# Convolution taps over five 64-token segments in two sums, sigmoids by tanh, and weight splits queued later at the second norm

## The chip, the core and the metric

The kernel runs on one core of a Trainium2 chip. The metric is the device time of one execution in microseconds (us). A core has a matrix engine (TensorE, PE in the profile, with its weight loads as PEld), VectorE (DVE), ScalarE (ACT), GpSimd (POOL) and a queue that starts transfers (SyncE, SP). Each engine runs its own instructions strictly in the order in which they were queued, and waits on semaphores for the others.

## The reference

One layer of a streaming encoder, for a prompt of 256 tokens and a running stream of 64 tokens that share the weights:

```python
h = rmsnorm(x, g_pre_mix);  p = h @ w_in
# head group A, 1024 channels: Conformer convolution
u = h_val * sigmoid(h_gate)
u = causal depthwise conv over positions, width 31 (w_dw, b_dw)   # prompt after zeros, stream after its state
u = silu(LayerNorm per token over each group of 128 channels)
# head group B, 8 heads of 128: gated DeltaNet (short conv of width 4, l2norm, beta = sigmoid(b_raw), delta rule in chunks of 64)
x = x + rmsnorm(concat(A, B) @ w_out)
h = rmsnorm(x);  gu = causal depthwise conv (width 3) of h @ w_up
x = x + rmsnorm((silu(gate) * up) @ w_down)
```

It also returns the convolution states (the last 30 rows of `u` among them) and the delta-rule states.

## The kernel before

Activations lie with channels on the 128 partitions and the 320 tokens (256 + 64) on the free axis. Every matrix product is done in three passes of 128x128 weights on 320 tokens: high part of the weight by high part of the activation (L212), high by low (L213), low by high (L216). The parts come from `split_w` (L192): a DMA lands 128x1024 weights in a buffer `w`, ACT copies it to `whi` (L196) and DVE subtracts to `wlo` (L197). There are three buffers each of `w`, `whi` and `wlo`.

The program is traced as one stream of dense matrix blocks. Small work is spread between them: `tick` counts dense matmuls, and every 20 (`GAP`) it resumes generators ("jobs": convolution tails, head tails, `pair` with `levels` and `post`) and takes up to `pace` convolution steps from the list `taps`. A list scheduler then orders each engine's queue by priorities, data and the `issue_after` edges; so an edit in one place also moves neighbours.

What the change touches:

- `gates` (L398): `beta` is a Sigmoid on ACT (L414).
- `conv_block` (L503), run eight times (c0 to c7): the gate block's `sg` is scaled on DVE (L508), goes through Sigmoid on ACT (L509) and is multiplied by `rb` on POOL (L510). The values go to `ub`, one row of 380 columns: 30 border columns, 256 tokens, 30 state columns (L515), 64 tokens. The 31 taps run over 350 of these columns. Tap 0 is on ACT (L525); taps 1 to 30 are one DVE instruction each that reads `cvt` and writes it again (L526), so each needs the result of the one before.
- `conv_tail` (L532): PE transposes `cvt` (`pt_c`, L541), DVE takes statistics (L543, L544), POOL the power (L547), DVE `gnm` (L549), ACT normalises into `un` (L552).
- `levels` (L731): PE forms `pz` (L741), DVE masks it into `zs` (L743), PE goes on with `px` from `zs` (L747). PE's queue holds L747 at a fixed place among the dense matmuls, so PE stands still if `zs` is late.
- the second norm (L1020 to L1042): after the last block of `w_out`, PE sums squares (L235), DVE and POOL make the root (`rr`, L240, L241), PE spreads it (L248) into `psb`, and fills the time with matmuls of zeros (`keep_warm`, L256). Then for each of 16 feature blocks k DVE does `m[k] * rb1` (L1036) and adds it to `x1` (L1037), ACT makes `hi2[k]` (L1041) and DVE `lo2[k]` (L1042); PE starts the first up-projection group (`up_group`, L1051) with block 0. The weights of that group are split by `up_weights` (L987), eight tiles of two blocks each, in between. In L1028 the third of these splits is tied behind `held`, an ACT instruction, only.

Of the kernel before, what the change touches and what calls it, by code (L numbers as in the profile page):

```python
# [12 lines left out]
ALU = mybir.AluOpType  # L13
# [88 lines left out]
def trunk_kernel(ctx, tc, ins, outs):  # L102
# [295 lines left out]
    def gates():  # L398
# [12 lines left out]
        S.copy(ba, ps3[:, :, 0:16])  # L411
        V.tensor_tensor(ba, ba, ps3[:, :, 16:32], ALU.add)
        beta = const.tile([P, 3, NH], F32, tag="beta", name="beta")
        S.activation(beta, ba[:, :, 0:8], AF.Sigmoid)  # L414
        gt = const.tile([P, 3, NH], F32, tag="gt", name="gt")
        dtb = gpar[:, 8:16].unsqueeze(1).to_broadcast((P, 3, NH))
        ax = small.tile([P, 3, NH], F32, tag="ax", bufs=1, name="ax")
# [74 lines left out]
    ubufs = [cb.tile([P, 380], F32, tag=f"ub{i}", bufs=1, name=f"ub{i}") for i in range(3)]
    for u in ubufs:
        G.memset(u[:, 0:30], 0.0)
# [8 lines left out]
    def conv_block(b):  # L503
        psg_ = in_block(8 + b, "psgate")
        ub = ubufs[b % 3]
        with tc.high_priority(offset=PRI_E):
            sg = cb.tile([P, T], F32, tag="sg", name="sg")
            V.tensor_tensor(sg, psg_[:, 0:T], rb, ALU.mult)  # L508
            S.activation(sg, sg, AF.Sigmoid)  # L509
            G.tensor_tensor(sg, sg, rb, ALU.mult)  # L510
        psv = in_block(b, "psv")
        if b > 2:
            finish_conv(b - 3)
        with tc.high_priority(offset=PRI_E):
            G.tensor_copy(ub[:, 286:316], pv("s_conv", b * 30, (b + 1) * 30))  # L515
            V.tensor_tensor(ub[:, 30:286], psv[:, 0:TP], sg[:, 0:TP], ALU.mult)
            V.tensor_tensor(ub[:, 316:380], psv[:, TP:T], sg[:, TP:T], ALU.mult)
        nc.sync.dma_start(outs["conv"][:, b, 0, :], ub[:, 256:286])
        nc.sync.dma_start(outs["conv"][:, b, 1, :], ub[:, 350:380])
        cvt = cb.tile([P, 350], F32, tag="cvt", bufs=3, name="cvt")  # L520
        left = [31]

        def tap(t):
            if t == 0:
                return lambda: S.activation(cvt, ub[:, 0:350], AF.Identity, scale=pv("w_dw", b * 31), bias=pv("b_dw", b))  # L525
            return lambda: V.scalar_tensor_tensor(cvt, ub[:, t:t + 350], pv("w_dw", b * 31 + t), cvt, ALU.mult, ALU.add)  # L526

        lefts[b] = left
        taps.extend((left, tap(t)) for t in range(31))
        return cvt, left  # L530

    def conv_tail(b, cvt, left):  # L532
        while left[0]:
            yield GAP, 0, 0
        yield LAG_CONV, 0, 1
        pt = ps_t.tile([P, 512], F32, tag="t", name="pt_c")
        st = cb.tile([P, 3, 6], F32, tag="bst", name="bst")
        gv = cb.tile([P, 3, 2], F32, tag="gvar", name="gvar")

        for c, o in enumerate((0, 128, 222)):  # L540
            PE.transpose(pt[:, c * P:(c + 1) * P], cvt[:, o:o + P], cv("ident"))  # L541
        for c in range(3):
            V.bn_stats(st[:, c, :], pt[:, c * P:(c + 1) * P])  # L543
            V.bn_aggr(gv[:, c, :], st[:, c, :])  # L544
        rs = cb.tile([P, 3], F32, tag="grs", name="grs")
        G.tensor_scalar(rs, gv[:, :, 1], EPS, None, ALU.add)
        G.tensor_tensor(rs, rs, nhalf[:, 0:3], ALU.pow)  # L547
        nm = cb.tile([P, 3], F32, tag="gnm", name="gnm")
        V.scalar_tensor_tensor(nm, gv[:, :, 0], -1.0, rs, ALU.mult, ALU.mult)  # L549
        un = cb.tile([P, 3, P], F32, tag="un", bufs=1, name="un")  # L550
# [471 lines left out]
    with tc.high_priority(offset=PRI_E):  # L1022
# [2 lines left out]
        keep_warm(psw, 5, mm)  # L1025
        rb1, mm = rstd_rows(rr)
        keep_warm(psw, 10, mm)
        with tc.issue_after(held):  # L1028
            upw.append(up_weights(2))
        for k in range(KB):  # L1030
            if k % 2 == 1 and 3 <= k < 13:
                upw.append(up_weights(len(upw)))
            with ExitStack() as e:
                if 0 < k < 4:
                    e.enter_context(tc.issue_after(added))
                V.tensor_tensor(m[k], m[k], rb1, ALU.mult)  # L1036
# [230 lines left out]
```

## Time and profile before

| | us |
|---|---|
| median of 3 runs | 1509.7 (1509.48 to 2070.93) |
| the profiled execution, its own time | 1506.6 |
| span of its trace | 1504.8 |
| PE busy in the span | 1490.6 |
| DVE busy | 1009.6 |
| ACT busy | 734.9 |
| POOL busy | 275.9 |

Busy time of PE is modelled and its matmuls overlap, so its share alone doesn't say how much is lost; the places where it stood idle, and the clock it was granted, do. Stage by stage: input projections with convolution and delta rule up to about 442 us, output projection to 552, second norm and first up-projection group to about 588, feed-forward to 1490, and a tail.

### The profile page before, as it was taken

The page shows a single profiled execution, that of the slowest core. Times are in us where ns is not written, and L with a number is a line of the kernel's source. Part 1 is how long each engine was busy: PE and PEld are TensorE (multiplying, and loading weights), DVE is VectorE, ACT ScalarE, POOL GpSimd, SP SyncE. Part 2 cuts the span into 40 slices and gives each one's busy share as a digit, 9 for nine tenths or more (in the row PEclk, how much of TensorE's full clock was granted, in tenths as well). Part 3 has the DMA queues.
Part 4 walks back from the last instruction along what each step waited for, and adds up shares of the span by engine and source line. Part 5 has one row for each costly group of instructions (what it writes and reads, how often), then busy time and mean ns, then how long its engine had stood idle before and what let it go on. Part 6 is the DMA issues. An engine that isn't in the chain of part 4 may idle for free.

```text
span 1504.8 us, 26707 instructions
## 1 busy us (share of the span) xinstructions
PE 1490.6 (99%) x10330; PEld 1469.6 (98%) x10330; DVE 1009.6 (67%) x1852; ACT 734.9 (49%) x1223; POOL 275.9 (18%) x459
## 2 busy tenths in 40 slices
PE   9999999999999999999999999999999999999998
PEld 9999999989999989999999999999999999999997
DVE  6798898879987578865435666545665545666554
ACT  7663656554555565544344444334444333444453
POOL 0322122330110000322002322001322101322101
PEclk9999999999999999999999999999999999999999
DMA  8435453445334653444555444455444455444453
GB/s 294 150 114 153 140 158 102 125 154 147 118 105 144 201 187 127 141 154 133 144 159 166 144 152 142 135 153 172 142 154 151 126 153 173 144 152 154 128 152 117
DMA packets 98279, 224.25 MB, mean 149 GB/s; under 512 B 18792, under 2 KB 39528, under 8 KB 98152
## 3 DMA queue, kind: packets, MB, share of 16 engines
q1 hardware_dynamic: 98008, 222.51, 47.5%
q8 instruction: 81, 1.33, 0.4%
q14 instruction: 46, 0.38, 0.1%
q10 hardware_dynamic: 144, 0.03, 0.0%
HBM read 215.39 MB, written 7.12 MB: 148 GB/s over the span
## 4 chain that ended last, share of the span: by engine, by line
PE 88%; DVE 6%; DMA 2%; ACT 2%; POOL 1%; issue 1%; ACTq 0%; DVEq 0%; SPq 0%; POOLq 0%
PE psu L212 13%; PE psu L213 13%; PE psu L216 13%; PE psdn L212 6%; PE psdn L213 6%; PE psdn L216 6%; PE psq L212 2%; PE psq L216 2%; PE psq L213 2%; DVE wlo L197 2%; DVE cvt L526 2%; PE psu L1060 2%; PE ps_first L374 1%; PE psgate L216 1%; PE psv L212 1%
## 5 line engine op out<-in xcount | busy, mean ns | idle before, releaser
L196 ACT CAST whi<-w 128x1024 fp32r<-128x1024 f32 (+2 forms) x440 | 412.2, 940 | 502.1 <-PE psu L213 170.1
L197 DVE TENSOR_TENSOR wlo<-w,whi 128x1024 fp32r<-128x1024 f32 (+2 forms) x440 | 477.3, 1085 | 187.1 <-ACT whi L196 114.1
L212 PE MATMUL psu<-hi,whi 128*128 128x320 f32 x1344 | 397.0, 309 | 0.0
L213 PE MATMUL psu<-lo,whi 128*128 128x320 f32 x1344 | 396.9, 309 | 0.0
L212 PEld LDWEIGHTS psu<-hi,whi 128*128 128x128 f32 x1344 | 252.3, 188 | 0.0
L213 PEld LDWEIGHTS psu<-lo,whi 128*128 128x128 f32 x1344 | 252.3, 188 | 0.0
L216 PE MATMUL psu<-hi,wlo 128*128 128x320 f32 x1344 | 224.4, 309 | 0.0
L1093 POOL COPY nffn<-fbuf 128x2 f32<-128x2 f32 x88 | 99.4, 1129 | 587.5 <-DVE fbuf L1091 583.0
L216 PEld LDWEIGHTS psu<-hi,wlo 128*128 128x128 f32 x1344 | 204.1, 188 | 0.0
L213 PE MATMUL psdn<-gl,whi 128*128 128x320 f32 x660 | 195.9, 310 | 0.0
L1091 DVE TENSOR_TENSOR fbuf<-psu,rb 128x256 f32<-128x256 f32 x88 | 37.4, 424 | 169.1 <-PE psu L216 169.0
L212 PE MATMUL psdn<-gh,whi 128*128 128x320 f32 x480 | 142.8, 309 | 0.0
L526 DVE SCALAR_TENSOR_TENSOR cvt<-ub,par,cvt 128x350 f32<-128x350 f32 x240 | 136.7, 587 | 2.9 <-ACT cvt L525 0.3
L213 PEld LDWEIGHTS psdn<-gl,whi 128*128 128x128 f32 x660 | 123.9, 188 | 0.3
L212 PE MATMUL psq<-hh,whi 128*128 128x320 f32 x352 | 106.1, 315 | 0.0
L213 PE MATMUL psq<-hl,whi 128*128 128x320 f32 x352 | 104.1, 309 | 0.0
L212 PEld LDWEIGHTS psdn<-gh,whi 128*128 128x128 f32 x480 | 90.1, 188 | 0.0
L216 PE MATMUL psdn<-gh,wlo 128*128 128x320 f32 x480 | 89.8, 309 | 0.0
L216 PEld LDWEIGHTS psdn<-gh,wlo 128*128 128x128 f32 x480 | 75.4, 188 | 0.0
L212 PEld LDWEIGHTS psq<-hh,whi 128*128 128x128 f32 x352 | 66.1, 188 | 0.3
L213 PEld LDWEIGHTS psq<-hl,whi 128*128 128x128 f32 x352 | 66.1, 188 | 0.2
L1136 DVE TENSOR_TENSOR y<-y,psdn 128x320 f32<-128x320 f32 x45 | 22.0, 489 | 58.4 <-PE psdn L216 58.4
(356 smaller groups left out, 2503.0 us busy)
## 6 DMA issues: line engine op xcount, KB each, us to landing
w<-in_w_up SPq DMA_DIRECT2D x176, 512.0 KB, 3.8
w<-in_w_in SPq DMA_DIRECT2D x88, 512.0 KB, 3.7
w<-in_w_down SPq DMA_DIRECT2D x64, 384.0 KB, 3.1
w<-in_w_down SPq DMA_DIRECT2D x64, 320.0 KB, 2.9
w<-in_w_out SPq DMA_DIRECT2D x32, 320.0 KB, 3.2
w<-in_w_out SPq DMA_DIRECT2D x16, 384.0 KB
w<-in_w_first SPq DMA_DIRECT2D x6, 512.0 KB, 5.8
wtp<-wsp SPq DMA_DIRECT2D x4, 640.0 KB
```

What stands on the lines that cost most here:

```text
L196: S.copy(hi[:, 0:width], w[:, 0:width])
L197: V.tensor_tensor(lo[:, 0:width], w[:, 0:width], hi[:, 0:width].bitcast(F32), ALU.subtract)
L212: tick(PE.matmul(ps, wh, xh, start=(first and k0 + j == 0), stop=False))
L213: tick(PE.matmul(ps, wh, xl, start=False, stop=False))
L216: tick(PE.matmul(ps, lo[:, j * P:(j + 1) * P], xh, start=False, stop=(final and k0 + j == nk - 1)))
L374: tick(PE.matmul(ps, w, xh, start=(k == 0 and wt is hi), stop=(k == KB - 1 and wt is lo)))
L526: return lambda: V.scalar_tensor_tensor(cvt, ub[:, t:t + 350], pv("w_dw", b * 31 + t), cvt, ALU.mult, ALU.add)
L1060: PE.matmul(pss[i][:, 0:T], wt[:, o:o + P], x, start=(k == 0 and n == 0), stop=(k == KB - 1 and n == 2))
L1091: V.tensor_tensor(buf[:, 2:258], psu[:, 0:TP], rb2[:, 0:TP], ALU.mult)
L1093: G.tensor_copy(nffn[:, b, 0, :], buf[:, 256:258])
L1136: V.tensor_tensor(y[:, n, :], y[:, n, :], psd[:, 0:T], ALU.add)
```

## The change

**Taps.** `ub` becomes five segments of 94 columns, 30 of border and 64 of tokens. One DVE instruction writes all five token parts, and a new POOL copy writes the borders of segments 1 to 3 from the ends of segments 0 to 2. Each tap covers 5x64 = 320 columns. Even taps add into `cvt`, odd taps into a new tile `odd` (one buffer); tap 1 is a plain multiply, and a 32nd step adds the two.

**Sigmoids.** `sigmoid(x)` becomes `0.5 * tanh(x / 2) + 0.5`: ACT computes Tanh, and a new POOL instruction scales and shifts, for `beta` and for each `sg` (now with one buffer).

**Second norm.** The splits of up-projection tiles 2, 3 and 4 are queued behind `lo2` of blocks 0, 2 and 4; those of tiles 5 to 7 stand at blocks 7, 9 and 11.

```diff
-        S.activation(beta, ba[:, :, 0:8], AF.Sigmoid)
+        S.activation(beta, ba[:, :, 0:8], AF.Tanh, scale=0.5)
+        G.tensor_scalar(beta, beta, 0.5, 0.5, ALU.mult, ALU.add)
...
-    ubufs = [cb.tile([P, 380], F32, tag=f"ub{i}", bufs=1, name=f"ub{i}") for i in range(3)]
+    ubufs = [cb.tile([P, 5, 94], F32, tag=f"ub{i}", bufs=1, name=f"ub{i}") for i in range(3)]
...
-            S.activation(sg, sg, AF.Sigmoid)
+            S.activation(sg, sg, AF.Tanh, scale=0.5)
+            G.tensor_scalar(sg, sg, 0.5, 0.5, ALU.mult, ALU.add)
             G.tensor_tensor(sg, sg, rb, ALU.mult)
...
-            G.tensor_copy(ub[:, 286:316], pv("s_conv", b * 30, (b + 1) * 30))
-            V.tensor_tensor(ub[:, 30:286], psv[:, 0:TP], sg[:, 0:TP], ALU.mult)
-            V.tensor_tensor(ub[:, 316:380], psv[:, TP:T], sg[:, TP:T], ALU.mult)
+            G.tensor_copy(ub[:, 4, 0:30], pv("s_conv", b * 30, (b + 1) * 30))
+            V.tensor_tensor(ub[:, :, 30:94], psv[:, 0:T].rearrange("p (s i) -> p s i", s=5),
+                            sg.rearrange("p (s i) -> p s i", s=5), ALU.mult)
+            G.tensor_copy(ub[:, 1:4, 0:30], ub[:, 0:3, 64:94])
...
-        left = [31]
+        cvt = cb.tile([P, 5, 64], F32, tag="cvt", bufs=3, name="cvt")
+        odd = cb.tile([P, 5, 64], F32, tag="odd", bufs=1, name="odd")
+        left = [32]
 
         def tap(t):
+            if t == 31:
+                return lambda: V.tensor_tensor(cvt, cvt, odd, ALU.add)
+            x, acc, w = ub[:, :, t:t + 64], (cvt, odd)[t % 2], pv("w_dw", b * 31 + t)
             if t == 0:
-                return lambda: S.activation(cvt, ub[:, 0:350], AF.Identity, scale=pv("w_dw", b * 31), bias=pv("b_dw", b))
-            return lambda: V.scalar_tensor_tensor(cvt, ub[:, t:t + 350], pv("w_dw", b * 31 + t), cvt, ALU.mult, ALU.add)
+                return lambda: S.activation(acc, x, AF.Identity, scale=w, bias=pv("b_dw", b))
+            if t == 1:
+                return lambda: V.tensor_scalar(acc, x, w, None, ALU.mult)
+            return lambda: V.scalar_tensor_tensor(acc, x, w, acc, ALU.mult, ALU.add)
...
-        with tc.issue_after(held):
-            upw.append(up_weights(2))
+        split = None
         for k in range(KB):
-            if k % 2 == 1 and 3 <= k < 13:
-                upw.append(up_weights(len(upw)))
+            if k % 2 == 1 and k < 13:
+                with ExitStack() as e:
+                    if k < 7:
+                        e.enter_context(tc.issue_after(split))
+                        e.enter_context(tc.issue_after(held))
+                    upw.append(up_weights(len(upw)))
...
-            V.scalar_tensor_tensor(lo2[k], x1[:, k, :], g, hi2[k].bitcast(F32), ALU.mult, ALU.subtract)
+            split = V.scalar_tensor_tensor(lo2[k], x1[:, k, :], g, hi2[k].bitcast(F32), ALU.mult, ALU.subtract).ins
```

In ACT's queue 18 of 27 loads of a function table go. PE keeps the same instructions in other places; DVE gets eight `tensor_scalar` and eight adds for eight taps and eight multiplies less; POOL gets 17 instructions more.

How the queues move, at three places. First DVE ahead of the mask of the third pair's `levels`, before (`qb` is a head's short convolution with its taps in `cq`, `psq` its matrix block):

```order
L526 SCALAR_TENSOR_TENSOR cvt<-ub_584,par,cvt 128x350 x4
L587 TENSOR_TENSOR qb_591<-psq,rb 128x256
L588 TENSOR_TENSOR qb_591<-psq,rb 128x64
L543 BN_STATS bst<-pt_c 128x6 x2
L544 BN_AGGR gvar<-bst 128x2
L543 BN_STATS bst<-pt_c 128x6
L594 SCALAR_TENSOR_TENSOR cq<-qb_591,par,cq 128x323
L544 BN_AGGR gvar<-bst 128x2 x2
L594 SCALAR_TENSOR_TENSOR cq<-qb_591,par,cq 128x323
L549 SCALAR_TENSOR_TENSOR gnm<-gvar,grs 128x3
L197 TENSOR_TENSOR wlo<-w,whi 128x1024
L594 SCALAR_TENSOR_TENSOR cq<-qb_591,par,cq 128x323
L743 TENSOR_TENSOR zs<-pz,cst 128x20x16
```

and after, in the same queue (L537 is the tap, L754 the mask; the line numbers of the changed file are higher by 11 here):

```order
L537 SCALAR_TENSOR_TENSOR cvt<-ub_584,par,cvt 128x320
L598 TENSOR_TENSOR qb_591<-psq,rb 128x256
L599 TENSOR_TENSOR qb_591<-psq,rb 128x64
L197 TENSOR_TENSOR wlo<-w,whi 128x1024
L605 SCALAR_TENSOR_TENSOR cq<-qb_591,par,cq 128x323
L537 SCALAR_TENSOR_TENSOR odd<-ub_584,par,odd 128x320
L605 SCALAR_TENSOR_TENSOR cq<-qb_591,par,cq 128x323
L537 SCALAR_TENSOR_TENSOR cvt<-ub_584,par,cvt 128x320
L605 SCALAR_TENSOR_TENSOR cq<-qb_591,par,cq 128x323
L754 TENSOR_TENSOR zs<-pz,cst 128x20x16
```

Five taps, `cvt` and `odd` in turn, stand ahead of the `qb` rows instead of four; behind them the statistics and `gnm` of a convolution tail have moved behind the mask, and two taps have come in. On PE the three transposes `pt_c` of that tail, ahead of `pz` before, now stand among the `px` of L747.

Second, ACT in the output projection, before (`whi` copies, `un` of a convolution tail, `m` the copies out of finished blocks):

```order
L955 COPY m6_5655<-psm_5591 128x320
L196 CAST whi_5761<-w_5759 128x640
L552 ACTIVATE un_5694<-pt_c_5677,gnm_5692,grs_5689 128x128 x3
L955 COPY m7_5732<-psm_5657 128x320
L196 CAST whi_5789<-w_5787 128x768
```

and after:

```order
L966 COPY m6_5673<-psm_5609 128x320
L196 CAST whi_5779<-w_5777 128x640
L196 CAST whi_5807<-w_5805 128x768
L966 COPY m7_5750<-psm_5675 128x320
L196 CAST whi_5835<-w_5833 128x640
L563 ACTIVATE un_5742<-pt_c_5725,gnm_5740,grs_5737 128x128 x3
```

The three `un` have moved behind two `whi` copies and `m7`.

Third, DVE at the second norm, before:

```order
L240 TENSOR_SCALAR rr_6650<-pst_6643 128x3
L197 TENSOR_TENSOR wlo_6675<-w_6672,whi_6674 128x1024
L1036 TENSOR_TENSOR m0_5254<-m0_5254,psb_6658 128x320
L197 TENSOR_TENSOR wlo_6699<-w_6696,whi_6698 128x1024
L1037 TENSOR_TENSOR x1_6131<-x1_6131,m0_5254 128x320
L1036 TENSOR_TENSOR m1_5333<-m1_5333,psb_6658 128x320
L197 TENSOR_TENSOR wlo_6717<-w_6714,whi_6716 128x1024
L1042 SCALAR_TENSOR_TENSOR lo2_0_6681<-x1_6131,par_81,hi2_0_6680 128x320
```

and after:

```order
L240 TENSOR_SCALAR rr_6675<-pst_6668 128x3
L1050 TENSOR_TENSOR m0_5272<-m0_5272,psb_6683 128x320
L1051 TENSOR_TENSOR x1_6156<-x1_6156,m0_5272 128x320
L1050 TENSOR_TENSOR m1_5351<-m1_5351,psb_6683 128x320
L1051 TENSOR_TENSOR x1_6156<-x1_6156,m1_5351 128x320
L1050 TENSOR_TENSOR m2_5403<-m2_5403,psb_6683 128x320
L1056 SCALAR_TENSOR_TENSOR lo2_0_6700<-x1_6156,par_81,hi2_0_6699 128x320
L197 TENSOR_TENSOR wlo_6706<-w_6703,whi_6705 128x1024
L1056 SCALAR_TENSOR_TENSOR lo2_1_6712<-x1_6156,par_81,hi2_1_6711 128x320
```

The three `wlo` that stood ahead of `lo2` of block 0 now come one behind each of `lo2` 0, 2 and 4; from there on every pair of blocks has one `wlo` in it until the eighth tile, where before the pairs between blocks 1 and 9 had none. ACT's three `whi` copies of these tiles stay ahead of `hi2` of block 0.

## Rows read from the trace of the kernel before

**Rows 1.** The page: busy us, share of the span and instructions of each engine.

```profile
PE 1490.6 (99%) x10330; PEld 1469.6 (98%) x10330; DVE 1009.6 (67%) x1852; ACT 734.9 (49%) x1223; POOL 275.9 (18%) x459
```

**Rows 2.** Waits of PE: us in total, times, longest.

```profile
PE px L747 <- DVE zs L743: 3.3, 2, 2.8
PE psm L212 <- ACT whi L196: 1.3, 1, 1.3
PE pks L670 <- ACT vh L662: 1.0, 1, 1.0
PE psm L1009 <- DVE wlo L197: 0.8, 1, 0.8
PE psu L1060 <- ACT hi L1041: 0.6, 1, 0.6
```

**Rows 3.** Windows: length, busy us (count) of PE, PEld, DVE, ACT, POOL, granted clock, DMA.

```profile
322.90:325.50 2.60, 2.60 (x20) 2.60 (x21) 2.53 (x4) 2.58 (x4) 0.00 (x0) 0.82 0.80 239
325.50:328.00 2.50, 2.50 (x11) 2.50 (x11) 2.02 (x5) 0.06 (x1) 0.00 (x0) 0.50 0.48 170
...
442.00:500.00 58.00, 56.74 (x392) 56.44 (x391) 40.25 (x80) 28.67 (x55) 5.76 (x13) 1.00 0.49 145
```

**Rows 4.** Timeline of DVE ahead of that wait: start, length, instruction, idle before.

```profile
302.17 0.59 DVE L526 SCALAR_TENSOR_TENSOR cvt<-ub,par,cvt 128x350 f32<-128x350 f32 x1
302.67 0.56 DVE L594 SCALAR_TENSOR_TENSOR cq<-qb,par,cq 128x323 f32<-128x323 f32 x1
...
307.87 1.82 DVE L526 SCALAR_TENSOR_TENSOR cvt<-ub,par,cvt 128x350 f32<-128x350 f32 x3
...
314.77 2.43 DVE L526 SCALAR_TENSOR_TENSOR cvt<-ub,par,cvt 128x350 f32<-128x350 f32 x4
317.12 0.42 DVE L587 TENSOR_TENSOR qb<-psq,rb 128x256 f32<-128x256 f32 x1
317.46 0.21 DVE L588 TENSOR_TENSOR qb<-psq,rb 128x64 f32<-128x64 f32 x1
317.59 0.48 DVE L543 BATCH_NORM_STATS2 bst<-pt_c 128x6 f32<-128x128 f32 x2
...
322.29 0.48 DVE L743 TENSOR_TENSOR zs<-pz,cst 128x320 f32<-128x320 f32 x1
```

**Rows 5.** Line L510 on POOL and the table load of L509: min/median/max ns.

```profile
L510 POOL TENSOR_TENSOR sg<-sg,rb x8: 862/1036/3268, 81.2 to 420.9; 128x320 f32<-128x320 f32 x8
L509 ACT ACT_TABLE_LOAD   x8: 1283/1283/1283, 79.4 to 419.1; - x8
```

**Rows 6.** Timeline around the wait of the output projection, 466 to 481 us.

```profile
469.36 0.49 PE L541 MATMUL pt_c<-cst,cvt 128*128 128x128 f32 x3
...
476.62 1.16 ACT L552 ACTIVATE un<-pt_c,gnm,grs 128x128 f32<-128x128 f32 x3 [5.27 <-DVE gnm L549]
...
477.97 2.22 ACT L196 CAST whi<-w 128x768 fp32r<-128x768 f32 x3
```

**Rows 7.** Timeline of the second norm, 545 to 566 us.

```profile
554.46 2.32 PE L256 MATMUL psw<-wz 128*128 128x512 bf16 x10
554.66 0.49 DVE L1036 TENSOR_TENSOR m<-m,psb 128x320 f32<-128x320 f32 x1
555.06 1.22 DVE L197 TENSOR_TENSOR wlo<-w,whi 128x1024 fp32r<-128x1024 f32 x1
556.20 0.48 DVE L1037 TENSOR_TENSOR x<-x,m 128x320 f32<-128x320 f32 x1
...
556.72 0.56 ACT L1041 ACTIVATE hi<-x,par 128x320 fp32r<-128x320 f32 x1 [1.46 <-DVE x L1037]
...
558.13 0.55 DVE L1042 SCALAR_TENSOR_TENSOR lo<-x,par,hi 128x320 fp32r<-128x320 f32 x1
558.60 0.48 DVE L1037 TENSOR_TENSOR x<-x,m 128x320 f32<-128x320 f32 x1
```

**Rows 8.** The chain in order of time: the rest of the first up-projection group.

```profile
559.73 26.68 PE psu L1060 x180
```

More of the change, by code (lines that the diff above doesn't have):

```diff
@@ L489, in trunk_kernel @@
     nqkv = const.tile([P, 24, 2, 3], F32, tag="nqkv", name="nqkv")
[L492 removed]
+    ubufs = [cb.tile([P, 5, 94], F32, tag=f"ub{i}", bufs=1, name=f"ub{i}") for i in range(3)]
     for u in ubufs:
[L494 removed]
+        G.memset(u[:, 0, 0:30], 0.0)
     def finish_conv(b):
@@ L514, in conv_block @@
         with tc.high_priority(offset=PRI_E):
-            G.tensor_copy(ub[:, 286:316], pv("s_conv", b * 30, (b + 1) * 30))
-            V.tensor_tensor(ub[:, 30:286], psv[:, 0:TP], sg[:, 0:TP], ALU.mult)
-            V.tensor_tensor(ub[:, 316:380], psv[:, TP:T], sg[:, TP:T], ALU.mult)
-        nc.sync.dma_start(outs["conv"][:, b, 0, :], ub[:, 256:286])
-        nc.sync.dma_start(outs["conv"][:, b, 1, :], ub[:, 350:380])
-        cvt = cb.tile([P, 350], F32, tag="cvt", bufs=3, name="cvt")
-        left = [31]
+            G.tensor_copy(ub[:, 4, 0:30], pv("s_conv", b * 30, (b + 1) * 30))
+            V.tensor_tensor(ub[:, :, 30:94], psv[:, 0:T].rearrange("p (s i) -> p s i", s=5),
+                            sg.rearrange("p (s i) -> p s i", s=5), ALU.mult)
+            G.tensor_copy(ub[:, 1:4, 0:30], ub[:, 0:3, 64:94])
+        for i in range(2):
+            nc.sync.dma_start(outs["conv"][:, b, i, :], ub[:, 3 + i, 64:94])
+        cvt = cb.tile([P, 5, 64], F32, tag="cvt", bufs=3, name="cvt")
+        odd = cb.tile([P, 5, 64], F32, tag="odd", bufs=1, name="odd")
+        left = [32]
         def tap(t):
+            if t == 31:
+                return lambda: V.tensor_tensor(cvt, cvt, odd, ALU.add)
+            x, acc, w = ub[:, :, t:t + 64], (cvt, odd)[t % 2], pv("w_dw", b * 31 + t)
             if t == 0:
-                return lambda: S.activation(cvt, ub[:, 0:350], AF.Identity, scale=pv("w_dw", b * 31), bias=pv("b_dw", b))
-            return lambda: V.scalar_tensor_tensor(cvt, ub[:, t:t + 350], pv("w_dw", b * 31 + t), cvt, ALU.mult, ALU.add)
+                return lambda: S.activation(acc, x, AF.Identity, scale=w, bias=pv("b_dw", b))
+            if t == 1:
+                return lambda: V.tensor_scalar(acc, x, w, None, ALU.mult)
+            return lambda: V.scalar_tensor_tensor(acc, x, w, acc, ALU.mult, ALU.add)
         lefts[b] = left
-        taps.extend((left, tap(t)) for t in range(31))
-        return cvt, left
+        taps.extend((left, tap(t)) for t in range(32))
+        return cvt.rearrange("p s i -> p (s i)"), left
     def conv_tail(b, cvt, left):
@@ L538, in conv_tail @@
         gv = cb.tile([P, 3, 2], F32, tag="gvar", name="gvar")
-        for c, o in enumerate((0, 128, 222)):
+        for c, o in enumerate((0, 128, 192)):
             PE.transpose(pt[:, c * P:(c + 1) * P], cvt[:, o:o + P], cv("ident"))
```

2 lines of the change are left out of this document (1 added, 1 removed).

## The prediction

> **What bounds the kernel now.** The first view is the page's busy time: PE is busy for 1490.6 of 1504.8 us [rows 1], and the change takes no instruction off it. A dense matmul costs 26.68 / 180 = 0.148 us from start to start [rows 8], so time can come or go only where PE stands still or runs at a lower clock. The second view, the waits of PE, names those places; with the first up-projection group they come to some 7 us [rows 2]: 3.3 us for the masks `zs` of `levels` (one wait of 2.8), 1.3 and 0.8 us in the output projection, 1.0 us in a head's tail, 0.6 us at the second norm. The third view, windows, adds the clock. [...] That makes 0.36 x 2.6 = 0.94 us and 2.5 us at half clock, and half of it is lost: **1.7 us**. So everything that can be won is about 9 us, 0.6% of the time. About 2% is what a measurement of this kernel can tell from no change, so whichever way the details go, the result should count as no change; the rest is about its size.
>
> **The taps.** DVE, not PE, is what the 2.8 us wait hangs on, so I follow its queue there [rows 4]. Three taps in a row take 1.82 us and four take 2.43: 0.61 us for each further one. A tap followed by an instruction that doesn't read its result costs only 302.67 - 302.17 = 0.50 us. The difference of 0.11 us is what waiting for the own result costs. The nearest row to a tap of 320 columns is `lo` at the second norm, also two tensors and a per-channel number: 558.60 - 558.13 = 0.47 us to an independent successor [rows 7]. With two sums a tap always follows one of the other sum, so I take 0.47; if two sums didn't help it would be about 0.61 - 0.03 = 0.58. That the 320 columns now lie in five pieces I cost at nothing: the mask `zs`, in pieces of 16 columns, takes 0.48 us for 320 columns [rows 4], no more than plain ones (0.48, rows 7).
>
> Now the queue to `zs`. The three taps ahead of 314.77 save 2 x 0.14 + 0.03 = 0.31 us. The four taps, 317.12 - 314.77 = 2.35 us, become five: 5 x 0.47 = 2.35, no difference. So the first `qb` row moves from 317.12 to 316.81. After it stand two `qb` rows (0.34 and 0.13), one `wlo` (556.20 - 555.06 = 1.14, rows 7), and then three `cq` and two taps, in turn, at 0.47 each: 0.34 + 0.13 + 1.14 + 2.35 = 3.96, so `zs` starts at 320.77 instead of 322.29, 1.5 us sooner. The statistics and the `gnm` of the convolution tail, which stood in between, now come later. So do three transposes on PE (0.49 for three, rows 6, about 0.4 from start to start), which came before the wait and now come behind it: the net gain is **1.1 us**, and the wait left is 2.8 - 1.5 + 0.4 = 1.7 us. Whether the clock still falls decides 1.7 us more. The wait of 2.8 was followed by the fall; the window of 442 to 500, which holds the wait of 1.3, shows 1.00 [rows 3]. 1.7 is nearer to 1.3 than to 2.8, so I take the clock to stay up: **1.7 us**, with none as the other end.
>
> The wait of 1.0 in a head's tail goes through `tq`, POOL and ACT, with three taps ahead of it on DVE: **0.3 us**. For the other 0.5 us of `zs` (3.3 - 2.8) I take nothing: four taps there become five, and a product for a head's output, which reads PE's result, has moved ahead of the mask; 0.5 either way.
>
> In the output projection ACT has waited 5.27 us for `gnm` when it starts three `un` at 476.62, and the `whi` that PE needs comes only at 477.97 [rows 6]: that is PE's 1.3 [rows 2]. In the changed queue that `whi` and one more stand ahead of the `un`, and nothing they need comes from DVE. **1.2 us**, between 0 (if the next `whi` behind `un` is late instead) and 1.3. The 0.8 us of L1009 hangs on a weight transfer; its place in SP's queue shifts by a position or so, which I cost at 0, with 0.8 either way.
>
> **The sigmoids.** A table load is 1.28 us [rows 5]; 18 of them are 23 us of ACT, which is busy half the time, and PE's waits on ACT are the two above. The new POOL instruction reads one tensor of 320 columns; L510, which reads two, takes 0.86 to 3.27 us [rows 5], the nearest row, and I take its median of 1.04. So `sg` is ready between 1.28 - 0.86 = 0.4 us sooner and 2.0 later. What hides it is the value block of 48 matmuls between `sg` and its use, 7.1 us; without that cover eight blocks would cost up to 16 us. On the path: **0**. The border copy on POOL is a new wait for tap 0 on ACT and tap 1 on DVE. Behind tap 0 stand `whi` copies, behind tap 1 the `wlo` and the work of the heads, which PE takes some microseconds later; if POOL is free it is short, and I take 0. It is the dearest risk (rival 2).
>
> L510's 3.27 us against a median of 1.04 [rows 5] shows that POOL can be held up; which instruction held it the row doesn't say. [...]
>
> **The second norm.** Before, DVE puts a `wlo` between `m[0]` and its addition: they start at 554.66 and 556.20, and `hi` starts at 556.72 and takes 0.56 [rows 7]. Without the `wlo` the addition starts 0.40 us behind `m[0]`, at 555.06, and `hi` at 555.06 + 0.52 = 555.58, done by 556.14. But PE's ten zero matmuls run from 554.46 to 556.78 [rows 7], so block 0 starts at about 556.6 instead of 557.3: 0.7 us. Then a pair of blocks costs PE 24 x 0.148 = 3.55 us, and DVE four steps at 0.40, two `lo` at 0.47 and one `wlo` at 1.14, 3.68 us: six pairs in a row lose 6 x 0.13 = 0.8 us, of which some 0.3 is covered by DVE's lead at the start. Net **0.2 us**, between 0.7 won and 0.6 lost (ACT's `whi` copies, 1.03 us each, now stand between the `hi` as well, and wait for a buffer that PE frees). SP's loads of the tiles behind it start later, when the splits free their buffers, but each tile is needed 3.55 us after the one before.
>
> **Sum.** 1.1 + 1.7 + 0.3 + 1.2 + 0.2 = 4.5 us. The profiled execution would take 1506.6 - 4.5 = 1502.1 us. The median lies 3.1 us above it; I put the change on the median: 1509.7 - 4.5 = **1505.2 us**.
>
> **Rivals.** 1. Two sums don't help: a tap costs 0.58, `zs` starts at 314.46 + 5 x 0.58 + 0.47 + 1.14 + 5 x 0.5 = 321.5, 0.8 us sooner; the net gain is 0.4, the wait left 2.4, and the clock falls as before. The sum is 0.4 + 1.2 + 0.2 = 1.8, and the time 1507.9. For it: nothing but this difference of 0.11 us in a few rows. [...]
>
> 2. Slower: the border copy. POOL serves in order, and where the copy stands behind a head's powers or the two `sg` steps, tap 0 waits for it on ACT with a `whi` behind it. At L510's longest, 3.27 us, less the lead of a `whi` (one tile, 24 x 0.148 = 3.55 us, of which casting and subtracting take 2.2), PE stands 1.9 us per block. It decides from a copy that is more than 1.4 us late; in five of eight blocks it costs 9.5 us, and 1509.7 - 4.5 + 9.5 = 1514.7. Against it: POOL is busy 275.9 of 1504.8 us [rows 1].
>
> 3. The other waits fall too: 0.5 of `zs`, 0.8 of L1009, all of the 1.0, and the 1.7 left: 4 us more, 1501.
>
> 4. The change doesn't do what it says at the second norm: DVE falls further behind and PE waits for `hi` from block 6 on, 1 us lost instead of 0.2 won: 1506.4. It lies within the forecast's own range.
>
> **Chances.** Forecast with rival 4, 1503 to 1507: 0.5. Rival 1, 1507 to 1510: 0.22. Rival 3, below 1503: 0.13. Rival 2, above 1510: 0.15. Leaving out the lower part of rival 3 and the upper part of rival 2, the range is **1500.5 to 1512.5**. None of the cases comes near 30 us: faster by over 2% 0.01, within 2% 0.97, slower by over 2% 0.02.
>
> **What would show it.** Taps on DVE 0.47 us apart; the wait of L747's successor near 320 us down to about 1.7, with a granted clock of 1.00 behind it; no wait of PE for `whi` at 477; the first block of the up-projection 0.7 us sooner behind the zero matmuls, and short waits for `hi` from block 6 on. The forecast is wrong if the clock still falls, if taps stay near 0.6 us apart, or if PE shows waits for `whi` or `wlo` behind the first taps of a block.

## The result and the profile after

| | before | after |
|---|---|---|
| median of the runs taken together (us) | 1510.53 (10 runs) | 1515.03 (10 runs) |
| the profiled execution, its own time | 1506.6 | 1512.55 |
| span of its trace | 1504.8 | 1510.8 |
| mean granted clock of the runs | 0.9975 (35 other runs) | 0.9952 |

The ratio is 1.0029, with an interval of 1.0020 to 1.0037: the changed kernel is 0.3% slower. One of the ten runs before took 2070.9 us and is left out of the ratio. The forecast was 0.3% faster, and its range ended at 1512.5. That 2% is what can be told from no change, as the prediction had it, is too coarse: the interval tells 0.3%. A mean clock lower by 0.0023 over 1512 us is 3.5 us lost, so by this estimate most of the 4.5 us is time at half clock.

The page's busy time, as in [rows 1]:

```profile
PE 1494.7 (99%) x10329; PEld 1472.2 (97%) x10330; DVE 1000.3 (66%) x1852; ACT 712.9 (47%) x1205; POOL 306.3 (20%) x476
```

DVE and ACT have 9 and 22 us less to do than before, POOL 30 more, and yet PE waits longer. The waits of PE (us in total, times, longest), to be held against [rows 2]:

```profile
PE px L758 <- DVE zs L754: 5.6, 2, 3.3
PE pks L681 <- ACT vh L673: 1.6, 1, 1.6
PE psw L256 <- POOL wz L226: 1.3, 1, 1.3
PE psm L212 <- ACT bh L220: 0.8, 1, 0.8
```

The wait for the mask `zs` was 3.3 us in all and is 5.6: the third `levels` waits 3.3 where 1.7 was forecast, and the fourth, which was put at no change, waits 2.3. The windows behind these two waits (columns as in [rows 3]):

```profile
324.00:326.30 2.30, 1.90 (x18) 1.90 (x19) 2.30 (x4) 1.48 (x3) 0.30 (x1) 1.00 0.48 185
326.30:329.70 3.40, 3.40 (x16) 3.40 (x16) 2.41 (x11) 0.00 (x0) 1.29 (x3) 0.50 0.51 154
397.50:404.90 7.40, 7.40 (x34) 7.40 (x35) 6.68 (x11) 1.82 (x4) 2.63 (x2) 0.54 0.20 71
404.90:430.00 25.10, 25.10 (x225) 23.99 (x225) 23.20 (x49) 10.93 (x21) 3.34 (x5) 1.00 0.33 101
```

The granted clock is 0.50 behind the first wait, for 3.4 us, and 0.54 in the mean behind the second, for 7.4 us. At the lower clock dense matmuls start 0.27 us apart (403.62, 403.89, 404.15, 404.42), at 1.00 behind it 0.15 (404.90, 405.05, 405.19). By the mean clock the first time costs 1.7 us, as before (0.50 from 324.6 to 328.0 there); the second is new and costs 7.4 x 0.46 = 3.4 us. Comparing the start of the same dense matmul in both traces, the changed kernel is behind by 0.4 us at 115 us, 1.1 at 318, 1.8 at 330, 1.9 at 390, 5.5 at 410, 7.4 at 436, 7.1 at 470, 5.9 at 500, 5.1 at 545, 4.1 at 560 and 5.9 from 620 to the end (times of the kernel before). So 3.6 us arise at the fourth `levels`, 1.9 between 410 and 436 (1.6 of it where PE waits for `bh` and `bl`), and 3.0 are given back between 470 and 560.

Why is the mask of the fourth `levels` late? DVE ahead of it, in the timeline:

```profile
382.69 1.23 DVE L197 TENSOR_TENSOR wlo<-w,whi 128x1024 fp32r<-128x1024 f32 x1 [2.27 <-ACT whi L196]
383.83 0.15 DVE L560 SCALAR_TENSOR_TENSOR gnm<-gvar,grs 128x3 f32<-128x3 f32 x1
383.90 0.54 DVE L536 TENSOR_SCALAR odd<-ub,par 128x320 f32<-128x320 f32 x1
384.35 0.54 DVE L537 SCALAR_TENSOR_TENSOR cvt<-ub,par,cvt 128x320 f32<-128x320 f32 x1
...
395.56 0.55 DVE L537 SCALAR_TENSOR_TENSOR cvt<-ub,par,cvt 128x320 f32<-128x320 f32 x1
396.02 0.55 DVE L537 SCALAR_TENSOR_TENSOR odd<-ub,par,odd 128x320 f32<-128x320 f32 x1
396.48 0.55 DVE L904 SCALAR_TENSOR_TENSOR zo<-pt_o,par,zT 128x320 f32<-128x320 f32 x1
396.94 0.48 DVE L754 TENSOR_TENSOR zs<-pz,cst 128x320 f32<-128x320 f32 x1
```

Taps start 0.46 us apart, as forecast. But DVE stands 2.27 us for a `whi`, and when it goes on, 19 taps are queued ahead of `zs`. Counted in DVE's rows from the start, 175 tap steps (the final additions among them) begin before this mask; in the kernel before there were 165. The `whi` is late because ACT is, and ACT because of POOL:

```profile
371.03 3.96 POOL L521 COPY ub<-ub 128x90 f32<-128x90 f32 x1 [3.89 <-DVE ub L519]
```

```profile
375.03 0.66 ACT L534 ACTIVATE cvt<-ub,par 128x320 f32<-128x320 f32 x1 [4.56 <-POOL ub L521]
375.59 1.03 ACT L196 CAST whi<-w 128x1024 fp32r<-128x1024 f32 x1
376.53 0.30 ACT L814 ACTIVATE vn<-ot 128x128 f32<-128x128 f32 x1
...
380.14 1.57 ACT L892 ACTIVATE ot<-ot,t 128x128 f32<-128x128 f32 x5 [2.92 <-POOL t L890]
381.62 1.03 ACT L196 CAST whi<-w 128x1024 fp32r<-128x1024 f32 x1
```

The border copy takes 3.96 us here (0.26 to 1.2 in the other seven blocks), while DVE runs a `wlo` and six taps back to back:

```profile
370.89 1.21 DVE L197 TENSOR_TENSOR wlo<-w,whi 128x1024 fp32r<-128x1024 f32 x1
372.02 0.54 DVE L537 SCALAR_TENSOR_TENSOR cvt<-ub,par,cvt 128x320 f32<-128x320 f32 x1
...
374.33 0.54 DVE L537 SCALAR_TENSOR_TENSOR odd<-ub,par,odd 128x320 f32<-128x320 f32 x1
```

ACT's tap 0 waits for the copy, with a `whi` and a head's tail behind it; the tail (`vn`, then POOL's `t`, then `ot`) holds up the `whi` that DVE waits for.

### The profile page after: what moved, and what is told of

Read it like the earlier page. It is cut to its first block, busy times and chain, and to the rows that moved or that the text cites. A ratio compares the mean times of both kernels' runs of the same rounds, so it can differ in the third digit from the quotient of the medians.

```text
span 1510.8 us, 26695 instructions
## 1 busy us (share of the span) xinstructions
PE 1494.7 (99%) x10329; PEld 1472.2 (97%) x10330; DVE 1000.3 (66%) x1852; ACT 712.9 (47%) x1205; POOL 306.3 (20%) x476
## 4 chain that ended last, share of the span: by engine, by line
PE 86%; DVE 7%; DMA 2%; ACT 2%; issue 1%; POOL 1%; SPq 0%; DVEq 0%; ACTq 0%
PE psu L216 13%; PE psu L213 13%; PE psu L212 13%; PE psdn L212 6%; PE psdn L213 6%; PE psdn L216 6%; DVE wlo L197 2%; PE psq L216 2%; PE psq L212 2%; PE psq L213 2%; PE psm L216 2%; PE psm L213 2%; PE psm L212 2%; PE psu L1074 1%; PE ps_first L374 1%
## 5 line engine op out<-in xcount | busy, mean ns | idle before, releaser
L537 DVE SCALAR_TENSOR_TENSOR cvt<-ub,par,cvt 128x320 f32<-128x320 f32 x120 | 66.4, 554 | 0.8 <-ACT cvt L534 0.6
L537 DVE SCALAR_TENSOR_TENSOR odd<-ub,par,odd 128x320 f32<-128x320 f32 x112 | 61.9, 553 | 0.0
```

The source lines that it names most:

```text
L537: return lambda: V.scalar_tensor_tensor(acc, x, w, acc, ALU.mult, ALU.add)
```

## The experiments

Each line of the table is one kernel, 4 to 12 runs of it. The ratio is to runs of the kernel before that were taken beside it; their median was 1509.4 to 1511.0 from group to group, so medians of different groups compare to within some 1.6 us.

| run | median us | ratio, interval |
|---|---|---|
| border_act | 1513.2 | 1.0018 (1.0009 to 1.0026) |
| taps_only | 1512.3 | 1.0011 (1.0002 to 1.0019) |
| tanh_only | 1511.2 | 1.0007 (0.9998 to 1.0015) |
| norm_only | 1511.1 | 1.0008 (0.9999 to 1.0017) |
| lag_after | 1508.3 | 0.9994 (0.9985 to 1.0003) |
| lag_before | 1511.7 | 1.0014 (1.0004 to 1.0023) |
| one_sum | 1510.9 | 1.0015 (1.0006 to 1.0023) |
| two_sums_350 | 1509.2 | 1.0002 (0.9993 to 1.0011) |
| taps_behind | 1506.6 | 0.9977 (0.9966 to 0.9988) |
| taps_behind_before | 1508.2 | 0.9982 (0.9973 to 0.9991) |
| two_only | 1507.6 | 0.9978 (0.9969 to 0.9988) |
| best | 1501.7 | 0.9945 (0.9932 to 0.9957) |
| norm_parts | 1503.2 | 0.9951 (0.9933 to 0.9969) |
| segments | 1506.1 | 0.9969 (0.9958 to 0.9980) |
| sigmoids | 1504.4 | 0.9956 (0.9940 to 0.9972) |
| one_row | 1508.9 | 0.9991 (0.9982 to 1.0001) |
| copy_on_act | 1502.7 | 0.9949 (0.9933 to 0.9966) |
| copy_on_dve | 1503.7 | 0.9956 (0.9941 to 0.9971) |

**First group: the copy, and each part alone.** border_act moves the border copy; the other three are the kernel before with the first, second or third group of hunks of the diff.

```diff
-            G.tensor_copy(ub[:, 1:4, 0:30], ub[:, 0:3, 64:94])
+            S.copy(ub[:, 1:4, 0:30], ub[:, 0:3, 64:94])
```

> The changed kernel with one edit: the copy of the segment borders runs on ACT, right ahead of tap 0, instead of on POOL. PE's order stays the same row for row. Theory A (the border copy: on POOL it took 3.96 us at 371.0 while six taps ran back to back on DVE; ACT's tap 0 waited 4.56 us for it, with a whi and a head's tail behind it, and so the mask zs came at 396.9): the wait of px near 395 falls from 2.45 us to below 1, the second stretch at half clock (6.8 us) is gone, and the time falls by 2.45 - 0.65 + 3.4 = 5.2 us, to about 1510. Theory B (DVE's queue is late because the scheduler put more taps ahead of the masks; the copy is by the way): the wait near 395 stays at 2 us or more and the time stays within 1 us of 1515. Theory C (POOL's new scalings of sg are what delays the blocks): as B, since they stay where they are.

> The kernel before with the change of the taps alone (five segments, two sums, border copy on POOL); sigmoids and the second norm as before. Theories A and B: the whole loss sits here. From PE's lag behind the kernel before at matched places of the two traces: 7.4 us by 438 us, less 2.3 us given back at the waits near 477 and 528, so about 5 us slower than before, some 1515.5 us, with a wait of px over 2 us near 395. Theory C: within 1 us of before (1510.5), since POOL's scalings are missing.

> The kernel before with sigmoids by tanh alone, 18 table loads gone from ACT and 9 scalings more on POOL. Theories A and B: within 1 us of before (1510.5), no new wait of PE over 1 us. Theory C: 3 to 6 us slower, with the multiplication of sg on POOL at 2 us or more in several blocks and waits of PE behind it.

> The kernel before with the second norm's splits moved, nothing else. By the prediction 0.2 us faster; by PE's lag in the changed kernel's trace (5.1 us at 545, 4.1 to 4.5 at 557 to 565, 5.9 at 606) 0.8 us slower, 1511.3: the first block comes about 0.7 us sooner, and DVE then loses some 1.5 us to PE over the next blocks. All three theories agree on it.

Theory A was half wrong. With the copy on ACT the median is 1.8 us lower, though the interval touches that of the changed kernel (1.0009 to 1.0026 against 1.0020 to 1.0037); `zs` came at 396.2, and PE still waited 2.2 us for it (2.3 in the changed kernel): with tap 0 out of the way, POOL's next instruction was held up instead.

```profile
375.28 2.23 POOL L887 TENSOR_TENSOR t<-t,so 128x5 f32<-128x5 f32 x1 [0.86 <-ACT vn L814]
377.59 0.21 POOL L888 TENSOR_SCALAR t<-t 128x5 f32<-128x5 f32 x1
```

A product of 128x5 took 2.23 us next to a `wlo`, two taps and the final addition, and ACT waited 4.16 us for the end of that chain, again with a `whi` behind. Theory C (the scalings) fell: they alone are within 1 us of before, and so are the moved splits. taps_only, expected at 1515.5, is 2.1 us slower than before, half of the loss. The three parts alone add up to 3.9 us by their medians, but none of them is large, and the intervals of two of them hold no change. The trace of norm_only says why such numbers are blurred. Up to 440 us its queues are those of the kernel before row for row, and yet its third `levels` waited 3.7 us instead of 2.8, and the clock was low for (1 - 0.63) x 14 / 0.5 = 10.4 us instead of 3.4:

```profile
323.00:337.00 14.00, 11.98 (x61) 11.97 (x62) 10.96 (x18) 6.27 (x21) 1.48 (x2) 0.63 0.36 112
```

The execution before that I had forecast from (1506.6 us, clock 0.999) was faster than every other run of that kernel.

**Second group: more time for the mask, and the two halves of the tap change.** The lag pair puts `px` 20 dense matmuls later, in the changed kernel and in the one before. one_sum keeps the segments with 31 taps in one sum. two_sums_350 keeps two sums on the old row of 350 columns, so without a border copy.

```diff
-        yield LAG_WAIT, 2, 0
+        yield LAG_WAIT + GAP, 2, 0
```

```diff
-            x, acc, w = ub[:, :, t:t + 64], (cvt, odd)[t % 2], pv("w_dw", b * 31 + t)
+            x, acc, w = ub[:, :, t:t + 64], cvt, pv("w_dw", b * 31 + t)
```

```diff
-            G.tensor_copy(ub[:, 1:4, 0:30], ub[:, 0:3, 64:94])
...
-            x, acc, w = ub[:, :, t:t + 64], (cvt, odd)[t % 2], pv("w_dw", b * 31 + t)
+            x, acc, w = ub[:, t:t + 350], (cvt, odd)[t % 2], pv("w_dw", b * 31 + t)
```

> The changed kernel with one edit: in levels, px is queued one step of 20 dense matmuls (3 us) later behind pz, so that the mask zs has that much longer. Theory K (mask and clock: the loss is PE's wait of px for zs at the third and fourth levels and the half clock that follows it; in norm_only, whose order up to 440 us is that of the kernel before row for row, the same place cost 3.9 us of wait and 10.2 us at half clock, so even the kernel before varies there): both waits, 5.6 us in sum, fall below 1, no half clock is left between 300 and 450 us (5.1 us lost there in the changed kernel's profile), and the time falls to 1506 to 1508. Theory P (POOL: taps back to back on DVE hold up POOL, and the loss is spread over the blocks behind its copies and powers): the two waits go, but others grow in their place, and the time stays above 1512.

> The same edit in the kernel before: px 20 dense matmuls later behind pz. Theory K: the wait of about 3 us and the half clock behind it (mean clock 0.9975 over 35 runs, 3.8 us lost, some 1 to 2 of it at the end where nothing waits) go, 1510.2 - 5 = 1505 us, and the distance to the changed kernel with the same edit is 2 us or less instead of 4.8. Theory P: both get shorter by the same amount, and the distance stays at 4 to 5 us.

> The changed kernel with the 31 taps in one sum again, on the five segments of 64; everything else as changed. The spacing of two taps in a row tells what the second sum is worth: 0.46 us with two sums; by the prediction about 0.58 with one. Theory K: DVE has 30 x 0.12 = 3.6 us more per block, zs comes later, 1515 us or more. Theory P: with gaps between the taps POOL gets through, the multiplication of sg and the border copy stay below 1.3 us, and the time falls to 1513 or less.

> The changed kernel with two sums over the old row of 350 columns: no segments and no border copy at all, PE's order the same row for row. Taps about 0.03 us dearer (0.49). Theory P, and the border copy as a part of it: as with the copy on ACT, 1513 us or less. Theory K: the copy matters only through the masks; zs as late as before, 1513 to 1516.

lag_after went nearly as theory K says, 6.8 us faster than the changed kernel by the medians (5.3 by the ratios), with the clock at 1.00 from 300 to 425 us; but a new wait for `bh` (2.7 us) came at 427, and the mean clock of the whole execution is 0.999. lag_before went against it: `zs` came 2.6 us later than before, with one tap more ahead of it, `px` still waited 1.7 us, `px` of the next step waited 2.7, and the kernel became slower. So "later" is no cure by itself. one_sum was faster than two sums on the segments, against K, although the taps of one sum stand further apart by the prediction's estimate (0.58 us, which no view of its trace shows, against 0.46 measured with two sums), and two_sums_350 was as fast as before, where K had 1513 to 1516. So the segments have a part in making the masks late. In the trace of two_sums_350 the third `levels` waited 1.8 us, and in lag_before 1.7, and both have a mean clock of 0.87, in these windows:

```profile
318.00:345.00 27.00, 25.16 (x203) 24.18 (x202) 19.38 (x48) 12.72 (x35) 6.97 (x12) 0.87 0.39 120
```

```profile
318.00:345.00 27.00, 25.29 (x196) 23.82 (x196) 19.51 (x44) 16.05 (x38) 5.10 (x11) 0.87 0.40 121
```

while border_act waited 2.9 us at the same place and has 1.00 there:

```profile
318.00:345.00 27.00, 24.13 (x220) 23.15 (x219) 21.76 (x52) 13.39 (x37) 7.46 (x12) 1.00 0.44 132
```

So in these three traces the length of the wait alone doesn't decide whether the clock falls.

**Third group: the mask ahead of the taps.** An edge keeps each tap that follows a mask in the program behind it in DVE's queue. PE's order stays but for a transpose or two. two_only is the kernel before with two sums on its own row alone, and best puts the good parts together: two sums on 350 columns, tanh, the second norm as before, and the edge.

```diff
-        with tc.issue_after(dense[0]):
+        with tc.issue_after(dense[0]), tc.issue_after(masked[0] or dense[0]):
             fn()
...
-        V.tensor_tensor(halves(zs, 0), pz.rearrange("p a (b w) -> p a b w", w=16), mask.unsqueeze(1).to_broadcast((P, NI, 4, 16)), ALU.mult)
+        masked[0] = V.tensor_tensor(halves(zs, 0), pz.rearrange("p a (b w) -> p a b w", w=16), mask.unsqueeze(1).to_broadcast((P, NI, 4, 16)), ALU.mult).ins
```

> The changed kernel with one edit: taps that come later in the program than a mask zs are kept behind it in DVE's queue (an order edge on each such tap); PE's order stays as it is but for the place of a transpose or two. Theory K (the loss is px waiting for zs, and the half clock that follows): zs of the third and fourth levels starts 1 to 3 us sooner, the two waits (3.5 and 2.5 us) shrink to 2 and 1 or less, the second half clock is gone, and the time falls by 3 to 6 us, to 1509 to 1512. A rival (the loss is in the blocks themselves, through POOL, and the waits would only move on): 1514 or more.

> The same edge in the kernel before. Theory K: the wait of 3 us at the third levels shrinks to 2 or less; with less half clock 1506 to 1508.5. By the rival no change, 1509 to 1511.

> The kernel before with two sums over its own row of 350 columns and nothing else of the change. If two sums are worth what the spacing says (0.49 instead of 0.61 us from tap to tap, some 3.5 us of DVE per block), zs comes 1 to 2 us sooner and the time is 1507 to 1509. If DVE's time is of no account there, 1509 to 1511. If the taps without gaps cost more through POOL than they win, above 1511.

> What the runs so far speak for, put together: two sums over the row of 350 columns without segments, sigmoids by tanh, the second norm as before, and later taps kept behind the masks. By theory K 1504 to 1507, faster than both kernels; by the rival 1508 to 1510, as two_sums_350.

This shows where the loss arises. The edge leaves segments, border copy and scalings as they are, and in the changed kernel it alone is worth 8.5 us by the medians (7.9 by the ratios), against 2.3 in the kernel before. In its trace 93 tap steps begin before the third mask and 146 before the fourth, instead of 121 and 175. By the starts of the same dense matmuls it wins 5.0 us by 330 and 9.7 by 410 (times of the changed kernel), and gives 2.3 back by the end. Its waits of PE no longer hold a `px` for `zs`, and the clock is 1.00 at both places:

```profile
PE pks L681 <- ACT vh L673: 1.7, 1, 1.7
PE psw L256 <- POOL wz L226: 1.3, 1, 1.3
PE pst L235 <- DVE acc L991: 0.6, 2, 0.4
```

```profile
318.00:330.00 12.00, 12.00 (x93) 11.99 (x93) 10.97 (x25) 5.78 (x21) 3.04 (x5) 1.00 0.47 147
388.00:405.00 17.00, 17.00 (x170) 16.52 (x169) 15.50 (x27) 7.53 (x13) 4.26 (x4) 1.00 0.46 145
```

With the edge on both sides the change is no longer slower than no change: 1506.6 against 1508.2, with intervals that overlap (0.9966 to 0.9988 and 0.9973 to 0.9991); without it, 4.5 slower. two_only, expected at 1507 to 1509, is 3.0 us faster than before without any edge, though its third `px` waited 2.2 us and its clock was 0.87 from 318 to 345: the second sum pays in the kernel before, on its own row. best beats both kernels, by 0.55% and, by the medians, 0.9%. Its five runs lie within 0.7 us (1501.4 to 1502.1), and in its trace the clock is 1.00 from 315 to 330, 385 to 405 and 450 to 560 us, and 1.0 in the mean of the execution.

**Fourth group: each part priced where less blurs it.** Parts are put into best or taken out of it. norm_parts puts in the third group of hunks, segments the first without the second sum (which best has), sigmoids takes tanh out, one_row the second sum (and gives `sg` its old buffers back).

> The kernel best with the change at the second norm put in. By the prediction 0.2 us faster than best (1501.5); by PE's lag in the traces with that change (start 0.7 to 1.1 us sooner, then 1.5 to 1.9 us lost by block 15) 0.5 to 1 us slower, 1502.2 to 1502.7.

> The kernel best with the taps on five segments of 64 and the border copy on POOL, as in the change; PE's order the same row for row. If segments cost only through late masks, which are now cured: within 0.5 us of best, 1501.2 to 1502.2. If the border copy on POOL delays heads by itself (3.96 us where DVE runs taps back to back): 1 to 4 us slower, 1503 to 1506, with waits of PE for ACT behind a tap 0.

> The kernel best with the Sigmoid activations back, 18 table loads more on ACT and 9 scalings less on POOL. By the prediction (both off the path) within 0.5 us of best; if ACT's 23 us of loads count, slower by 1 to 3 us.

> The kernel best with one sum over the row of 350 columns: taps 0.61 us apart instead of 0.49, some 3.5 us of DVE more per block. If the second sum is what lets DVE keep up: px waits for zs again by 1 us or more, the clock falls in some executions, 1504 to 1509. If not, within 1 us of best.

Against the 1501.7 of best, on the same chip: the second norm's splits cost 1.5 us, the segments with their copy 4.5; tanh is worth 2.7 and the second sum 7.2. These are prices of an edit with all that it moves. In one_row no long `px` wait is back, but PE waits 3.2 us for a `cvt` that isn't finished, and the mean clock of the execution is 0.998 (1.0 in best). In sigmoids 3.0 us arise between 332 and 338 us, at a wait that best doesn't have; DVE's queue holds two products `ub` ahead of the copy `zq` there, behind it in best:

```profile
335.35 0.33 DVE L769 COPY zq<-pz 32x160 f32<-32x160 f32 x1
```

```profile
PE px L774 <- DVE zq L769: 0.8, 1, 0.8
PE px L774 <- ACT zq L769: 0.6, 1, 0.6
```

The mean clock of this execution is 0.998 (1.0 in best). That ACT's table loads are the reason isn't shown. How the moved splits lose shows in the chain of norm_parts (start, us, what; long pieces from 562 to 575 us):

```profile
563.40 1.06 ACT whi L196
564.49 1.22 DVE wlo L197
565.71 0.46 DVE lo L1056
566.61 0.57 ACT hi L1055
567.23 3.80 PE psu L1074 x24
571.09 1.06 ACT whi L196
572.17 1.22 DVE wlo L197
```

A `whi` waits for a buffer that PE frees, the `wlo` waits for it on DVE, and behind that stand `lo`, the addition and so the next `hi`: per pair of blocks one round trip through three engines.

**Fifth group: is it the copy or the order of the taps?** The copy of segments goes to ACT (same diff as border_act; PE and DVE keep their orders row for row) or to DVE (`V.tensor_copy`).

> The kernel segments with the border copy on ACT right ahead of tap 0 instead of on POOL; the orders of PE and DVE are the same row for row. If POOL's copy is what costs (ACT waited 13.6 us for it at six tap 0): 2 to 4 us faster than segments, 1502 to 1504. If the segments cost through the order of DVE's taps: 1506 as segments.

> The kernel segments with the border copy on DVE behind the product. If POOL's copy is what costs: as with the copy on ACT, 1502 to 1504; DVE takes 8 x 0.2 us more, spread over the mixer. If the order of DVE's taps is what costs: anything, since this edit moves 85 of DVE's rows.

By the medians, the kernel is 3.4 us faster with the copy on ACT than on POOL (1506.1 to 1502.7; 3.0 by the ratios), and 2.5 faster with it on DVE. On ACT it takes 0.27 to 0.33 us in the eight blocks, on POOL up to 3.97:

```profile
L521 ACT COPY ub<-ub x8: 267/269/328, 86.8 to 427.4; 128x90 f32<-128x90 f32 x8
```

```profile
L521 POOL COPY ub<-ub x8: 258/1048/3967, 86.9 to 430.7; 128x90 f32<-128x90 f32 x8
...
  ACT cvt L534: 13.6, 6
```

The first is copy_on_act, the second segments (ns, least, median and most), with the 13.6 us that ACT's tap 0 waited for it. The two kernels ran on different chips; their runs don't overlap but for one of segments (1503.5).

How much of this is the slow copy stays open. By the starts of the same matmuls copy_on_act is ahead by 3.7 us at the end, and 2.5 of them arise between 108 and 116 us. They follow a `whi` that waited for its weights ahead of the first border copy, 2.18 us in segments and 0.92 in copy_on_act:

```profile
86.63 1.05 ACT L196 CAST whi<-w 128x1024 fp32r<-128x1024 f32 x1 [2.18 <-DMA w<-in_w_in]
```

```profile
85.30 1.05 ACT L196 CAST whi<-w 128x1024 fp32r<-128x1024 f32 x1 [0.92 <-DMA w<-in_w_in]
```

In segments PE then waits 2.3 us for `vh` (1.4 in copy_on_act), and the mean clock of its execution is 0.999 (1.0 in copy_on_act). At the copy of 3.97 us, from 369 to 415, the distance stays at 2.4 to 2.5; some 1.4 us come later.

## Why the prediction was wrong, point by point

1. **"Now the queue to `zs`" (1.1 us) is the step that failed.** The price of a tap was right: 0.46 us measured for 0.47, and two sums are worth 7.2 us in best. So was the replay from the first of the five taps to `zs`, 6.3 us forecast and 6.2 measured. What failed is that I replayed DVE's queue from the time at which DVE had come to 314.77 in the old trace. In the changed kernel it came there 2.9 us later, with PE 1.1 late, and `zs` started 1.6 later than before instead of 1.5 sooner; the wait grew from 2.8 to 3.3 us:

```profile
317.63 0.54 DVE L537 SCALAR_TENSOR_TENSOR cvt<-ub,par,cvt 128x320 f32<-128x320 f32 x1
...
323.86 0.49 DVE L754 TENSOR_TENSOR zs<-pz,cst 128x320 f32<-128x320 f32 x1
```

Two things stood ahead of that place. First, more taps: counted from the start, 121 tap steps begin before the third mask instead of 112 (three of the nine are final additions). Second, waits that DVE's speed doesn't end: from 225 to 325 us it stood 3.4 us for `sg` (0.3 before) and 2.4 for `bl` (not in the list before), while those for `tq` and `sc` fell only from 7.6 to 5.5. Why PE itself was 1.1 late there isn't traced.

```profile
DVE sg L510 <- PE psgate L216: 3.4, 1, 3.4
DVE bl L221 <- ACT bh L220: 2.4, 1, 2.4
```

Rival 1, that two sums don't help, fell: 0.46 us from tap to tap in the changed kernel, where it put 0.58.

2. **The clock (1.7 us).** It fell as before (0.50 over 3.4 us, 1.7 lost), and a second time (0.54 over 7.4 us). "1.7 is nearer to 1.3 than to 2.8" had no ground: behind waits of 1.7 us (lag_before) and 1.8 (two_sums_350) the clock was 0.87 in the mean from 318 to 345, behind one of 2.9 (border_act) 1.00. In lag_after, taps_behind and best, where PE has no wait for `zs` of over 0.4 us there, it is 1.00 at these places; no run shows more of what it hangs on. A term that only rests on a guess between two waits should have stood as a rival with even chances.

3. **The fourth `levels`, "0.5 either way", was mis-sized:** 1.8 us of wait more and 3.4 us lost at the lower clock (0.54 over 7.4 us). The sentence looked at the four or five taps directly ahead; the delay came from farther back: ten more tap steps ahead of the mask, and a `whi` that ACT and POOL held up. Taking tap 0 out of that chain (border_act) brought `zs` only 0.8 us sooner. The wait in a head's tail (`pks`), forecast to shrink from 1.0 by 0.3, grew to 1.6.

4. **The border copy, taken as 0, was not free,** though its price is open: 3.4 us by the medians of copy_on_act and segments, of which the two traces put most at another place. Rival 2 had the chain that the trace shows: POOL late, tap 0 waiting on ACT, a `whi` behind it. But I weighed it by POOL's busy share of 18%, which says nothing here: POOL was free, and its copy was slow beside what DVE did in the same 4 us. In the changed kernel's trace it came in one block and not in five. That rival 2's 1514.7 lies so near the measured 1515.0 is luck: it was added up from 1.9 us in each of five blocks, and the trace has the loss at two masks and in the clock behind them.

5. **The copy beside the taps.** The copy of 3.96 us ends at 371.03 + 3.96 = 374.99, just behind the last of six taps that run back to back (374.33 + 0.54 = 374.87). In this stretch GpSimd alone paid, since the taps kept their 0.46 us. What held the copy isn't shown: the overlap is all that the trace has, and no run separates a cause. The forecast had put the copy at nothing.

6. **The output projection (1.2 us) was right:** the lag goes from 7.1 to 5.9 there, and the wait for `whi` is gone from PE's list. The 0.8 of L1009, taken as 0, went too (0.2 left).

7. **The second norm (0.2 us).** The start was won, 1.0 us instead of 0.7. DVE's rate was mis-sized: 1.9 us are lost behind it instead of 0.5. I counted 3.68 us of DVE against 3.55 of PE per pair; in fact DVE's `wlo` waits for a `whi` that waits for PE's buffer, the end that I had named and not priced. The net is 0.9 us lost in the changed kernel's trace, which is rival 4 (1 us lost) in mechanism and size; norm_parts puts it at 1.5.

8. **The sigmoids, taken as 0,** held where other waits set the end (tanh_only is within 1 us of before), but in best tanh is worth 2.7 us. The trace of sigmoids has them at the waits for `zq` (0.8 and 0.6 us), where DVE's order differs, and a mean clock of 0.998 against 1.0 in best; whether ACT's loads count is not shown.

9. **"The median lies 3.1 us above it; I put the change on the median."** The profiled execution before was the fastest of all; its mean clock was 0.999, against 0.9975 over 35 other runs. With runs from 1507.9 to 1514.5, one trace doesn't tell this kernel's time to 5 us.

What stays open is what decides whether the clock falls behind a wait, what the slow copy costs by itself, and why one sum on segments (1510.9) beat two (1515.0) where nothing holds the masks. There one_sum has 113 tap steps ahead of the third mask and 167 ahead of the fourth, nearly as before, against 121 and 175; but two_sums_350, with 120 and 171, is as fast as before, so the number alone doesn't decide.

## What to carry to other kernels

When one engine waits at a fixed place for another's queue, fix the order at that place (an edge that keeps filler work behind the critical step) before making the filler cheaper: here the edge was worth 8.5 us in the changed kernel. The second sum brought 3.0 us without it (two_only) and 7.2 in best, the tanh nothing without it and 2.7 in best. A small step moved to an engine that is idle most of the time is not free if it then stands in front of a queue that others wait for; look at what runs beside it, not at its busy share (here one copy took from 0.26 to 3.96 us). And price parts on the version that repeats best: best spread by 0.7 us, the kernel before by 6.6 (35 runs, 1507.9 to 1514.5). Then look in the traces where the difference arises; a difference of medians doesn't say it.

## What the runs showed of the hardware

Two taps in a row start 0.46 us apart at 320 columns in the changed kernel, where the second adds into the other sum. At 350 columns, in the kernel before, a tap that reads the result of the one ahead of it starts 0.61 us behind it, and an instruction that doesn't 0.50 [rows 4]; with two sums on this row (two_sums_350) taps start 0.49 to 0.50 apart. Five pieces of 64 columns cost no more than one row: 0.46 us against 0.47 for `lo`, 320 columns in one piece [rows 7]. GpSimd instructions took up to fifteen times as long beside a run of taps: the copy of 128x90 takes from 0.26 to 3.96 us in the changed kernel, a product of 128x5 0.20 us at the least in the kernel before and 2.23 in border_act, while the taps beside the copy kept their 0.46. And the clock fell behind some waits of 1.7 us (0.87 in the mean from 318 to 345, lag_before) and not behind others of 2.9 (1.00, border_act), differently in executions of the same queues (3.4 us at 0.50 in before; 0.63 over 14 us in norm_only, which makes 10.4 us at 0.50, behind the same mask).
